# Keys, values and outputs of a delta-rule layer: turned by TensorE, or in 32x32 blocks by VectorE with DMAs through DRAM

## The chip, the cores and the metric

The kernel runs on one core of one Trainium2 chip. The metric is the device time of one execution in microseconds (us). Engines are named as the profile names them: PE (TensorE, matmuls; PEld its weight loads), DVE (VectorE), ACT (ScalarE), POOL (GpSimd) and SP (SyncE, which only issues DMAs here).

## The reference

A decoder trunk of two residual layers on 512 tokens of width 2048, in float32. The first layer is differential attention. The second, which the change touches, is a gated RWKV-7 mixer: 32 heads of 64, each with a 64x64 matrix state that is updated token by token.

```python
p = h @ w_in
p = p + (token_shift(p) - p) * mu
r, k, v, g, dw, da = jnp.split(p, RW_SPLITS, axis=-1)
...
def step(S, inp):
    r_t, w_t, k_t, v_t, a_t, b_t = inp
    sa = jnp.einsum('bhvk,bhk->bhv', S, a_t)
    S = S * w_t[:, :, None, :] + sa[..., None] * b_t[:, :, None, :] + v_t[..., None] * k_t[:, :, None, :]
    y = jnp.einsum('bhvk,bhk->bhv', S, r_t)
    return S, y
...
y = (y - mean) * lax.rsqrt(var + GN_EPS)
y = y * gn_w.astype(F32).reshape(RW_HEADS, RW_HEAD_DIM) + gn_b.astype(F32).reshape(RW_HEADS, RW_HEAD_DIM)
y = y + jnp.sum(rh * kh * r_k.astype(F32), axis=-1, keepdims=True) * vh
y = y.reshape(B, T, RW_WIDTH).astype(h.dtype) * jax.nn.silu(g)
return y @ w_out, v_first
```

## The kernel before

**Precision and projections.** Every large product is three matmuls (`mm3`, line 124) on parts of 32-bit numbers: high x high, high x low, low x high. A weight tile of 512 KB is loaded by SP (`load_w`, line 78) into one of three buffers `wraw`, ScalarE makes the high part `wh` (line 105), VectorE the low part `wl` (line 106), two buffers each, and TensorE runs 24 matmuls with the pair of parts.

**The second layer by pairs.** `layer1` walks over 16 blocks of 128 channels, two heads each, called pairs. In the loop's iteration j four projections run: values of pair j, keys of j + 1, gate of j - 2, receptances of j + 1. Channels lie on the partitions, the 512 tokens along the row. The recurrence is worked in eight chunks of 64 tokens. For a pair, `stage1` and `stage2` make the decays, the queries `AR` and the keys `BK` (its last write is line 1317). `gram` multiplies keys by queries (line 1361) and sends the lower triangles to DRAM (`ltd`, lines 1350 and 1373, on SP). `t_solve` loads them back on the GpSimd queue (`LT`, line 1407) and inverts them by substitution on VectorE (lines 1409 to 1429). The result goes out to `td` (line 1430) and back into `TT` (line 1449), both on SP, is turned in 32x32 blocks by VectorE (`T`, line 1459) and completed by small matmuls (lines 1465 and 1476).

**The chain.** The sequential scan of pair j - 1 (`scan_pair`) runs during iteration j, its matmuls set between those of the projections: each projection matmul counts one `tick`, and after a given number the generator goes one step on. A scan step c, one for each chunk, has three short products (lines 1558, 1569, 1576) with ScalarE copies and a VectorE update between them. At given steps it also calls a function of the dictionary `others`: in the iterations from j = 4 on, at step 0 `turn_keys(p, 0)` and `finish_y` of pair j - 2, at step 1 `turn_keys(p, 4)`, at step 2 `turn_values`; at step 4 and 6 go pieces of pair j's solve, at step 6 also `weigh`, which calls `gated`. After the last step come the outputs (lines 1598, 1602), `centre`, and in the next iteration `group_norm`, which leaves the normed outputs in `yc` and used the buffer `ysq` for squares.

**The three turns.** The scan wants keys, values and outputs with the axes swapped, 128x128 at a time. `turn_keys` makes four TensorE transposes into a PSUM bank (line 1393) and one ScalarE copy into `BKT` (line 1394, two buffers), twice a pair. `turn_values` makes four (line 1502) and four copies into `VS` (line 1506, two buffers). `finish_y` makes four of `yc` (line 1637), and VectorE scales the bank and adds it to `y` (line 1639). `gated` multiplies `y` by the gate (line 1531) and sends it to DRAM.

**What sets the order.** A scheduler puts the instructions of each engine in order, by priority and by when it reckons their inputs to be ready. A priority is the place in the program less an offset: 2000 for weight splits and loads, 3000 for what a chain step calls, 4000 or more for the solve. `issue_after` binds only instructions of the same engine to a place, so chain steps bind their matmuls to the tick, but not their VectorE work or DMAs. Each engine and each DMA queue then works in that fixed order: SP's queue carries the weights, `ltd`, `td` and `TT`, and whatever waits at its head holds up all behind it.

Of the kernel before, what the change touches and what calls it, by code (L numbers as in the profile page):

```python
# [13 lines left out]
F32 = mybir.dt.float32  # L14
# [4 lines left out]
ALU = mybir.AluOpType  # L19
# [4 lines left out]
P = 128  # L24
D = 2048
T = 512
KT = D // P
NT = T // P
# [13 lines left out]
def ahead(offset):  # L42


    def deco(f):
        def g_(g, *a, **k):
            with g.tc.high_priority(offset=offset):
                return f(g, *a, **k)

        return g_  # L50

    return deco
# [1139 lines left out]
C = 64  # L1192
NC_ = T // C
HALF = 32
NG = 4
# [55 lines left out]


class Pair:
    pass


def mus(g, i, j):
# [130 lines left out]
def turn_keys(g, p, c0):  # L1388

    nc = g.nc  # L1390
    ps = g.ps.tile([P, 512], F32, name="pt", tag="pb", bufs=2)
    for i in range(4):
        nc.tensor.transpose(ps[:, i * P : (i + 1) * P], p.BK[:, c0 + i].rearrange("p s t -> p (s t)"), g.ident[:])  # L1393
    nc.scalar.copy(p.BKT[:, c0 : c0 + 4], ps[:].rearrange("p (c k) -> p c k", c=4))


@ahead(SOLVE)
def t_solve(g, j, p, split):


    nc, w = g.nc, g.work
    NQ = HALF // NG
    LT = w.tile([P, HALF + 1, HALF], F32, name="LT", tag="LT", bufs=1)
    Tm = w.tile([P, NQ, HALF], F32, name="Tm", tag="Tm", bufs=1)
    tmp = w.tile([P, NQ * HALF], F32, name="tmpl", tag="tmpl", bufs=1)
    for i in range(NG):
        ld = nc.gpsimd.dma_start(out=LT[i * 32 : i * 32 + 32], in_=g.ltd[j % 2].rearrange("b h c s t -> (b h c) s t"))
    n2 = LT[:, HALF, :]
    nc.vector.tensor_scalar(n2, n2, 1e-24, None, ALU.max)
    nc.vector.reciprocal(n2, n2)  # L1410
    nc.gpsimd.memset(Tm[:], 0.0)
    tf = Tm[:].rearrange("p q t -> p (q t)")
    for i in range(NG):
        nc.gpsimd.memset(tf[i * 32 : i * 32 + 32, i :: HALF + NG], 1.0)

    def steps(a, b):
        for i in range(a, b):
            n, s = HALF - 1 - i, i // NG + 1
            tt = tmp[:, : n * s].rearrange("p (a b) -> p a b", a=s)
            nc.vector.scalar_tensor_tensor(tt, LT[:, i : i + 1, i + 1 :].to_broadcast([P, s, n]), n2[:, i : i + 1],  # L1420
                                           Tm[:, 0:s, i : i + 1].to_broadcast([P, s, n]), ALU.mult, ALU.mult)
            nc.vector.tensor_add(Tm[:, 0:s, i + 1 :], Tm[:, 0:s, i + 1 :], tt)  # L1422

    def parts():
        for a, b in zip(PARTS, PARTS[1:]):
            with g.tc.high_priority(offset=SOLVE), g.tc.issue_after(g.state.ins) if a and split else ExitStack():
                steps(a, b)
                if b == HALF - 1:
                    g.solved = nc.vector.tensor_mul(Tm[:], Tm[:], n2[:, None, :].to_broadcast([P, NQ, HALF])).ins
                    nc.sync.dma_start(out=g.td[j % 2].rearrange("q l t -> l q t"), in_=Tm[:])  # L1430
            if split:
                yield

    p.solve = parts()
    next(p.solve, None)
    return ld.ins
# [91 lines left out]


def gated(g, j, p, gt):  # L1530
    g.nc.vector.tensor_mul(gt[:], gt[:], p.y[:])
    g.nc.gpsimd.dma_start(out=g.yd2[j * P : (j + 1) * P, :], in_=gt[:])

# [85 lines left out]
def group_norm(g, j, p):  # L1619
    p.chain.finish(g)  # L1620
    nc, w, yc = g.nc, g.work, p.yc
    NG = 2 * NT
    sq = w.tile([P, NG, C], F32, name="ysq", tag="ysq", bufs=1)
    nc.scalar.activation(sq[:], yc[:], AF.Square)
    var = g.small.tile([P, NG], F32, name="var", tag="var", bufs=3)
    nc.vector.reduce_sum(var[:], sq[:], AX.X)
    nc.vector.tensor_scalar(var[:], var[:], 1.0 / C, GN_EPS, ALU.mult, ALU.add)
    rs = g.small.tile([P, NG], F32, name="rsg", tag="rsg", bufs=3)
    rsqrt(g, rs[:], var[:], NG, "r8")
    nc.vector.tensor_mul(yc[:], yc[:], rs[:, :, None].to_broadcast([P, NG, C]))  # L1630
# [11 lines left out]
def layer1(g, aps):  # L1642
    nc, tc = g.nc, g.tc
    with ExitStack() as cx:
# [3 lines left out]
        w = g.work  # L1648
        pairs = []
# [26 lines left out]
        r = receptances(0)  # L1676
        for j in range(D // P):
            p = pairs[j]
            if j:
                others = [(0, lambda p=p: turn_keys(g, p, 0)), (1, lambda p=p: turn_keys(g, p, 4)),  # L1680
                          (2, lambda p=p: turn_values(g, p))]
                if j > LAG + 1:
                    others[0] = (0, lambda p=p, i=j - 2: (turn_keys(g, p, 0), finish_y(g, i, pairs[i])))
                elif j > 1:
                    others.append((3, lambda i=j - 2: finish_y(g, i, pairs[i])))
                full = LAG < j < D // P - 1
                if full:
                    others += [(4, lambda p=p: next(p.solve)), (6, lambda p=p: (next(p.solve), weigh()))]
                gaps = ((6, 8) if j > LAG + 1 else (5, 6)) if full else (4, 4) if j > LAG else (4, 5)
                leads = {1: 72, LAG: 18, LAG + 1: 42}  # L1690
                chain(g, j - 1, pairs[j - 1], 5, *gaps, others, leads.get(j, GAP_D - GAP_T)).step(g)
            stage2(g, j, r, p)
            normed = j > LAG + 1 and pairs[j - 2].chain.wait is None
            if normed:
                group_norm(g, j - 2, pairs[j - 2])

            def behind(m, j=j, p=p, normed=normed):
                if j > 1:
                    pairs[j - 2].chain.finish(g)
                with tc.issue_after(m.ins):  # L1700
                    gram(g, j, p, j > LAG + 1 and pairs[j - 1].chain)
                with tc.issue_after(g.lower) if normed else ExitStack():
                    p.rfs = split_act(g, p.rf[:], w, "x")
                mask_gram(g, p, 0)
                loaded = t_solve(g, j, p, LAG < j < D // P - 1)
                with tc.issue_after(loaded):
                    mask_gram(g, p, 1)
                if j > 1 and not normed:
                    group_norm(g, j - 2, pairs[j - 2])

            stage_v(g, j, p, proj(2, j, behind=(24 if j == 1 else 18, behind)))
            if j == 0:
                turn_keys(g, p, 0)
                turn_keys(g, p, 4)
                Chain(g, first_values(g, p), 20)
            if j == 1:
                first = gate_of(0, "g0")
            if j + 1 < D // P:
                begin(j + 1)
            if j > LAG:  # L1720
                weights.append((j - LAG, gate(g, j - LAG, proj(3, j - LAG), later=True)))
            if j + 1 < D // P:
                r = receptances(j + 1)
            weigh()
            if j == LAG:
                gated(g, 0, pairs[0], first)
# [54 lines left out]
        for nm in ("11", "21", "22", "12"):  # L1781
            t, c = PLACES[nm]
# [21 lines left out]
@with_exitstack  # L1804
def body(ctx, tc, nc, aps):
    g = Ctx()
    g.nc, g.tc = nc, tc
    g.last, g.first, g.centred = None, [], None
    g.chains, g.later, g.state, g.copied = [], [], None, None
    g.const = ctx.enter_context(tc.tile_pool(name="const", bufs=1))  # L1810
    g.small = ctx.enter_context(tc.tile_pool(name="small", bufs=2))
    g.hp = ctx.enter_context(tc.tile_pool(name="hp", bufs=16))
    g.wraw = ctx.enter_context(tc.tile_pool(name="wrawp", bufs=3))
    g.wh = ctx.enter_context(tc.tile_pool(name="whp", bufs=2))
    g.wl = ctx.enter_context(tc.tile_pool(name="wlp", bufs=2))
    dr = ctx.enter_context(tc.tile_pool(name="dr", bufs=1, space=DRAM))
    g.ys = [dr.tile([D - 256, T], F32, name=f"ys{i}") for i in range(2)]
    g.yd2 = dr.tile([D, T], F32, name="yd2")
    g.xd = aps["x1"] if "x1" in aps else dr.tile([T, D], F32, name="xd")
    g.ltd = dr.tile([2, 2, 2, NC_, HALF + 1, HALF], F32, name="ltd")  # L1820
    g.td = dr.tile([2, HALF // NG, P, HALF], F32, name="td")
    g.ident = g.const.tile([P, P], F32, name="ident")
    g.fixed = g.const.tile([P, 16], F32, name="fixed")
    g.neglam, g.subw = g.fixed[:, 0:1], g.fixed[:, 1:3]
    make_identity(nc, g.ident)
    for n, layer in ((4, layer0), (2, layer1)):
        with tc.tile_pool(name="pp", bufs=n, space=PSUM) as g.pp, \
                tc.tile_pool(name="ps", bufs=1, space=PSUM) as g.ps:
            layer(g, aps)
# [42 lines left out]
```

## Time and profile before

| | us |
|---|---|
| median of 3 runs | 2054.83 (2054.38 to 2057.75) |
| profiled execution | 2055.6 |
| its span, first to last instruction | 2053.9 |
| PE busy | 2035.2 |
| VectorE busy | 1605.9 |
| ScalarE busy | 1133.6 |
| GpSimd busy | 400.3 |

The second layer's pairs run from about 950 to 1900 us of the span, one pair in some 59 us (line 1393's first transposes of a pair start at 1233.44, 1292.38, 1351.31, ...). How to read the profile: busy time is a sum over instructions of one engine, where overlapping matmuls count once; a row of the groups is "line engine operation out<-in shapes xcount | busy us, mean ns | idle time before them and who ended it"; a row of the timeline is "start us, duration us, engine line operation out<-in xcount [idle before <- releaser]"; a row of the windows has the stretch, its length, each engine's busy time with the number of instructions, the granted clock of TensorE (1.00 is full), the share of the DMA engines' time, and GB/s; a row of one line's instructions has min/median/max in ns, then first and last start. DMA issues by SP have no landing time in this trace; those by GpSimd have one.

### The profile page before, as it was taken

The page shows a single profiled execution, that of the slowest core. Times are in us where ns is not written, and L with a number is a line of the kernel's source. Part 1 is how long each engine was busy: PE and PEld are TensorE (multiplying, and loading weights), DVE is VectorE, ACT ScalarE, POOL GpSimd, SP SyncE. Part 2 cuts the span into 40 slices and gives each one's busy share as a digit, 9 for nine tenths or more (in the row PEclk, how much of TensorE's full clock was granted, in tenths as well). Part 3 has the DMA queues.
Part 4 walks back from the last instruction along what each step waited for, and adds up shares of the span by engine and source line. Part 5 has one row for each costly group of instructions (what it writes and reads, how often), then busy time and mean ns, then how long its engine had stood idle before and what let it go on. Part 6 is the DMA issues. An engine that isn't in the chain of part 4 may idle for free.

```text
span 2053.9 us, 34174 instructions
## 1 busy us (share of the span) xinstructions
PE 2035.2 (99%) x11922; PEld 1673.1 (81%) x11922; DVE 1605.9 (78%) x4100; ACT 1133.6 (55%) x2258; POOL 400.3 (19%) x782
## 2 busy tenths in 40 slices
PE   9999999999999999999999999999999999999999
PEld 7888888888888888888877778888888888877887
DVE  7988988888898977476787888787777888777745
ACT  5765656666666544355565555555555555545423
POOL 1020111102011000121222222322222222231011
PEclk9999999999999999999999999999999999999999
DMA  8487978879787965823333323223333232346676
GB/s 288 156 163 192 182 172 186 164 192 167 190 180 171 274 218 172 175 87 108 103 83 92 94 77 98 92 89 98 98 98 98 87 96 83 111 127 201 212 182 145
DMA packets 159534, 297.76 MB, mean 145 GB/s; under 512 B 64529, under 2 KB 81937, under 8 KB 159361
## 3 DMA queue, kind: packets, MB, share of 16 engines
q1 hardware_dynamic: 110768, 184.39, 28.8%
q0 software_dynamic: 25952, 90.88, 23.2%
q10 hardware_dynamic: 22640, 20.30, 3.1%
q8 instruction: 94, 1.54, 0.3%
q14 instruction: 80, 0.65, 0.1%
HBM read 271.33 MB, written 24.18 MB: 144 GB/s over the span
## 4 chain that ended last, share of the span: by engine, by line
PE 90%; DVE 6%; ACT 2%; issue 1%; DMA 1%; SPq 0%; ACTq 0%; DVEq 0%
PE pp L124 45%; PE pp L574 24%; PE pt L124 5%; PE gp L1361 2%; DVE wl L106 2%; PE sm L1558 1%; PE sc L124 1%; PE o L124 1%; PE sm L1576 1%; PE sm L1569 1%; ACT wh L105 1%; PE Y L1598 1%; PE pt L296 1%; PE z L124 1%; PE pt L1393 1%
## 5 line engine op out<-in xcount | busy, mean ns | idle before, releaser
L106 DVE TENSOR_TENSOR wl<-wraw,wh 128x1024 fp32r<-128x1024 f32 (+1 forms) x286 | 349.7, 1223 | 167.7 <-ACT wh L105 157.0
L105 ACT CAST wh<-wraw 128x1024 fp32r<-128x1024 f32 (+1 forms) x286 | 299.5, 1047 | 237.6 <-PE pp L124 115.8
L124 PE MATMUL pp<-hL,wh 128*128 128x512 f32 x1024 | 413.6, 404 | 0.0
L124 PE MATMUL pp<-hH,wl 128*128 128x512 f32 x1024 | 413.0, 403 | 0.0
L124 PE MATMUL pp<-hH,wh 128*128 128x512 f32 x1024 | 412.3, 403 | 0.2 <-ACT wh L105 0.2
L124 PEld LDWEIGHTS pp<-hH,wh 128*128 128x128 f32 x1024 | 193.1, 189 | 34.5 <-ACT wh L105 0.4
L124 PEld LDWEIGHTS pp<-hL,wh 128*128 128x128 f32 x1024 | 193.1, 189 | 33.5
L124 PEld LDWEIGHTS pp<-hH,wl 128*128 128x128 f32 x1024 | 193.2, 189 | 32.4
L574 PE MATMUL pp<-wh,hH 128*128 128x512 f32 x448 | 176.8, 395 | 0.0
L574 PE MATMUL pp<-wh,hL 128*128 128x512 f32 x448 | 175.8, 392 | 0.0
L124 PE MATMUL pp<-wh,hH 128*128 128x512 f32 x376 | 147.0, 392 | 0.6 <-ACT hH L1147 0.6
L124 PE MATMUL pp<-wl,hH 128*128 128x512 f32 x376 | 147.5, 392 | 0.0
L124 PE MATMUL pp<-wh,hL 128*128 128x512 f32 x376 | 147.3, 392 | 0.1
L1420 DVE SCALAR_TENSOR_TENSOR tmpl<-LT,Tm 128x60 f32<-128x60 f32 (+24 forms) x496 | 134.8, 272 | 13.2
L574 PE MATMUL pp<-wl,hH 128*128 128x512 f32 x448 | 140.3, 392 | 0.0
L1564 POOL COPY SA<-VS 64x64 f32<-64x64 f32 x224 | 55.4, 248 | 397.8 <-DVE VS L1580 375.4
L1422 DVE TENSOR_TENSOR Tm<-Tm,tmpl 128x60 f32<-128x60 f32 (+24 forms) x496 | 103.4, 209 | 11.7
L1561 ACT COPY rhs<-sm 64x64 f32<-64x64 f32 x256 | 53.0, 207 | 84.8 <-PE sm L1558 81.8
L574 PEld LDWEIGHTS pp<-wl,hH 128*128 128x128 f32 x448 | 84.5, 189 | 17.2
L574 PEld LDWEIGHTS pp<-wh,hH 128*128 128x128 f32 x448 | 84.2, 188 | 17.5 <-issue 0.4
L574 PEld LDWEIGHTS pp<-wh,hL 128*128 128x128 f32 x448 | 84.3, 188 | 16.1
L1571 ACT COPY VS<-sm 64x64 f32<-64x64 f32 x256 | 52.9, 207 | 76.2 <-PE sm L1569 70.3
(435 smaller groups left out, 4374.4 us busy)
## 6 DMA issues: line engine op xcount, KB each, us to landing
wraw<-in_rw_w_in_dram SPq DMA_DIRECT2D x128, 512.0 KB
wraw<-in_da_w_in_dram SPq DMA_DIRECT2D x75, 512.0 KB
wraw<-in_da_w_in_dram POOLq DMA_DIRECT2D x28, 512.0 KB, 6.6
wraw<-in_da_w_out_dram SPq DMA_DIRECT2D x26, 512.0 KB
wraw<-in_rw_w_out_dram SPq DMA_DIRECT2D x24, 512.0 KB
Ta<-in_da_w_in_dram POOLq DMA_DIRECT2D x21, 512.0 KB, 5.6
Tb<-in_da_w_in_dram POOLq DMA_DIRECT2D x21, 512.0 KB, 5.7
Tc<-in_da_w_in_dram POOLq DMA_DIRECT2D x21, 512.0 KB, 5.5
```

What stands on the lines that cost most here:

```text
L105: a = nc.scalar.copy(hi[:, ks], raw[:, ks])
L106: d = nc.vector.tensor_sub(lo[:, ks], raw[:, ks], hi[:, ks].bitcast(F32))
L124: m = nc.tensor.matmul(out, a, b, start=s, stop=e, skip_group_check=skip)
L296: nc.tensor.transpose(pt[:, c * P : (c + 1) * P], t1s[t][:, c * P : (c + 1) * P], g.ident[:])
L574: m = nc.tensor.matmul(out[t][:], x, wt[lo][:, k, :], start=first, stop=end and lo == 1 and k == KG - 1, skip_group_check=True)
L1361: m = nc.tensor.matmul(gp[h][:, i * P : (i + 1) * P], BK[r_, c0 + i, :, :], p.AR[r_, c0 + i, :, :], start=True, stop=True)
L1393: nc.tensor.transpose(ps[:, i * P : (i + 1) * P], p.BK[:, c0 + i].rearrange("p s t -> p (s t)"), g.ident[:])
L1420: nc.vector.scalar_tensor_tensor(tt, LT[:, i : i + 1, i + 1 :].to_broadcast([P, s, n]), n2[:, i : i + 1], Tm[:, 0:s, i : i + 1].to_broadca ...
L1422: nc.vector.tensor_add(Tm[:, 0:s, i + 1 :], Tm[:, 0:s, i + 1 :], tt)
L1561: nc.scalar.copy(rhs[r_, :], sm[r_, h * C : h * C + C])
L1564: nc.gpsimd.tensor_copy(p.SA[r_, c - 1, :], VS[r_, c, h, :])
L1571: g.copied = nc.scalar.copy(VS[r_, c, h, :], sm[r_, P : P + C])
```

## The change

In the iterations j = 4 to 15 the three functions are replaced by others that use no TensorE. `send_keys` turns each half of the pair's keys in 32x32 blocks with one VectorE transpose of 128x512, which leaves the blocks themselves at the wrong places. With the second half done, four DMAs on SP write the blocks to their places in a DRAM tile, and a fifth reads the whole back into `BKT`. `send_values` does the same for values (one transpose, four writes, two read-backs into `VS`, with `VS` itself as the buffer of the turned blocks), `send_y` for outputs (one transpose into `ysq`, four writes, one read-back). The writes go in pieces of 32 numbers, 128 bytes. The multiply-add that ended `finish_y` becomes a function `settle`, called at scan step 5, or by `gated` if it was not called until then. Pairs 0 to 3 for keys and values, and 0, 1, 14 and 15 for outputs, stay as before. Step 0 calls the first half of the keys and the outputs, step 1 the second half, step 2 the values.

```diff
+def halves_of(x):
+    return x.rearrange("(b r) t (q k) -> q r t b k", b=4, q=4)
+
+def send_keys(g, j, p, c0):
+    nc = g.nc
+    row = lambda x: x[:, c0 : c0 + 4].rearrange("p c k -> p (c k)")
+    nc.vector.transpose(row(p.BKT), p.BK[:, c0 : c0 + 4].rearrange("p c s t -> p (c s t)"))
+    if c0:
+        for q in range(4):
+            nc.sync.dma_start(out=halves_of(g.bkd[j % 2])[q],
+                              in_=p.BKT[q * 32 : q * 32 + 32].rearrange("r c (b k) -> r c b k", b=4))
+        nc.sync.dma_start(out=p.BKT[:], in_=g.bkd[j % 2])
+
+def send_values(g, j, p):
+    nc = g.nc
+    p.VS = g.work.tile([P, NC_, 2, C], F32, name="VS", tag="VS", bufs=2)
+    turned = p.VS[:].rearrange("p c h n -> p (c h n)")[:, 0:T]
+    nc.vector.transpose(turned, p.v[:])
+    for q in range(4):
+        nc.sync.dma_start(out=g.vd[j % 2, q // 2].rearrange("(b r) c (n k) -> n r c b k", b=2, n=2)[q % 2],
+                          in_=turned[q * 32 : q * 32 + 32].rearrange("r (c b k) -> r c b k", c=NC_, b=2))
+    for h in range(2):
+        nc.sync.dma_start(out=p.VS[(1 - h) * C : (2 - h) * C, :, h, :], in_=g.vd[j % 2, h])
+
+def send_y(g, j, p):
+    nc = g.nc
+    flat_ = lambda x: x[:].rearrange("p g n -> p (g n)")
+    nc.vector.transpose(flat_(p.sq), flat_(p.yc))
+    for q in range(4):
+        nc.sync.dma_start(out=halves_of(g.ytd[j % 2])[q],
+                          in_=flat_(p.sq)[q * 32 : q * 32 + 32].rearrange("r (t b k) -> r t b k", t=NT, b=4))
+    nc.sync.dma_start(out=flat_(p.sq), in_=g.ytd[j % 2].rearrange("p t k -> p (t k)"))
+
+    def settle():
+        p.settle = None
+        nc.vector.scalar_tensor_tensor(p.y[:], flat_(p.sq), g.prm["hgw"][:, j : j + 1], p.y[:], ALU.mult, ALU.add)
+
+    p.settle = settle
...
 def gated(g, j, p, gt):
+    if p.settle:
+        p.settle()
     g.nc.vector.tensor_mul(gt[:], gt[:], p.y[:])
...
                 if j > LAG + 1:
-                    others[0] = (0, lambda p=p, i=j - 2: (turn_keys(g, p, 0), finish_y(g, i, pairs[i])))
+                    others = [(0, lambda p=p, i=j - 2: (send_keys(g, i + 2, p, 0), send_y(g, i, pairs[i]))),
+                              (1, lambda p=p, j=j: send_keys(g, j, p, 4)), (2, lambda p=p, j=j: send_values(g, j, p)),
+                              (5, lambda i=j - 2: pairs[i].settle and pairs[i].settle())]
...
+    g.bkd = dr.tile([2, P, NC_, P], F32, name="bkd")
+    g.vd = dr.tile([2, 2, C, NC_, C], F32, name="vd")
+    g.ytd = dr.tile([2, P, NT, P], F32, name="ytd")
```

More of the change, by code (lines that the diff above doesn't have):

```diff
@@ L1253 @@
 class Pair:
-    pass
+    settle = None
 def mus(g, i, j):
@@ L1622, in group_norm @@
     NG = 2 * NT
-    sq = w.tile([P, NG, C], F32, name="ysq", tag="ysq", bufs=1)
+    sq = p.sq = w.tile([P, NG, C], F32, name="ysq", tag="ysq", bufs=1)
     nc.scalar.activation(sq[:], yc[:], AF.Square)
```

## The prediction

> **What bounds the kernel now.** I read the page first: busy time by engine and the chain that ended last.
>
> ```profile
> span 2053.9 us, 34174 instructions
> PE 2035.2 (99%) x11922; PEld 1673.1 (81%) x11922; DVE 1605.9 (78%) x4100; ACT 1133.6 (55%) x2258; POOL 400.3 (19%) x782
> ...
> PE 90%; DVE 6%; ACT 2%; issue 1%; DMA 1%; SPq 0%; ACTq 0%; DVEq 0%
> ```
>
> TensorE works in 99% of the span and carries 90% of the chain. A page's average may hide stages, so next come the windows, cut at one pair's period inside the changed stretch (1174 to 1822 us, where pairs 4 to 15 are prepared).
>
> ```profile
> 1292.00:1351.00 59.00, 59.00 (x428) 48.90 (x427) 46.51 (x129) 32.75 (x75) 15.00 (x37) 1.00 0.32 95
> ```
>
> In this 59 us the columns are PE 59.00, weight loads 48.90, VectorE 46.51, ScalarE 32.75, GpSimd 15.00, granted clock 1.00, DMA share 0.32. TensorE never rests; every other engine has room. Time taken off TensorE here should come off the kernel, as long as nothing new stops it.
>
> How much is that time? The busy time of overlapping matmuls is modelled, so I go by starts in TensorE's timeline. First a scan step without transposes, then three steps of one pair with them: step 0 (keys' first half and outputs), step 1 (keys' second half), step 2 (values).
>
> ```profile
> 1204.38 0.38 PE L1576 MATMUL sm<-VS,BKT 128*128 128x128 f32 x2
> 1204.52 0.48 PE L124 MATMUL pp<-hL,wh 128*128 128x512 f32 x1
> ...
> 1233.22 0.38 PE L1576 MATMUL sm<-VS,BKT 128*128 128x128 f32 x2
> 1233.44 0.60 PE L1393 MATMUL pt<-ident,BK 128*128 128x128 f32 x4
> 1233.88 0.60 PE L1637 MATMUL pt<-ident,yc 128*128 128x128 f32 x4
> 1234.23 0.48 PE L124 MATMUL pp<-hH,wl 128*128 128x512 f32 x1
> ...
> 1239.85 0.49 PE L1393 MATMUL pt<-ident,BK 128*128 128x128 f32 x3
> 1240.18 0.39 PE L1576 MATMUL sm<-VS,BKT 128*128 128x128 f32 x2
> ...
> 1240.43 0.47 PE L124 MATMUL pp<-hL,wh 128*128 128x512 f32 x1
> ...
> 1245.57 0.41 PE L1576 MATMUL sm<-VS,BKT 128*128 128x128 f32 x2
> 1245.82 0.60 PE L1502 MATMUL pt<-ident,mixv 128*128 128x128 f32 x4
> 1246.17 0.48 PE L124 MATMUL pp<-hH,wh 128*128 128x512 f32 x1
> ```
>
> Without transposes the projection follows the state product by 0.14 us (1204.38 to 1204.52). With eight it follows by 1.01 (1233.22 to 1234.23), which is 0.87 more. In step 1 the sequence takes 0.58 from the first transpose (1239.85 to 1240.43) where 0.14 would do: 0.44. In step 2 it takes 0.60: 0.46.
>
> **The change part by part.**
>
> *TensorE loses the transposes.* In the iterations j = 4 to 15 all sixteen of a pair go: eight of keys and four of values of pair j, four of outputs of pair j - 2. By the starts that is 0.87 + 0.44 + 0.46 = 1.77 us a pair, and 12 x 1.77 = 21.2 us. The other end is the busy sum:
>
> ```profile
> L1393 PE MATMUL pt<-ident,BK 128*128 128x128 f32 x128 | 20.7, 273 | 0.0
> L1637 PE MATMUL pt<-ident,yc 128*128 128x128 f32 x64 | 9.7, 274 | 1.0 <-DVE yc L1630 1.0
> L1502 PE MATMUL pt<-ident,mixv 128*128 128x128 f32 x64 | 9.6, 272 | 0.0
> ```
>
> 96 of 128, 48 of 64 and 48 of 64 go, three quarters of 40.0 us: 30.0. I take 21.2, because a start-to-start difference is what the next matmul really waited, while the busy sum counts overlap with it. 30.0 stays as the far end of the gain.
>
> *VectorE gains four transposes of 128x512 a pair,* two for keys, one each for values and outputs. The trace has one of 64x256, and a cheap small operation:
>
> ```profile
> L1459 DVE STREAM_TRANSPOSE T<-TT x32: 425/440/443, 1003.3 to 1868.1; 64x256 f32<-64x256 f32 x32
> ...
> L1409 DVE TENSOR_SCALAR LT<-LT x16: 172/181/183, 963.4 to 1831.2; 128x32 f32<-128x32 f32 x16
> ...
> L1639 DVE SCALAR_TENSOR_TENSOR y<-pt,prm_hgw,y x16: 742/751/752, 1079.7 to 1916.7; 128x512 f32<-128x512 f32 x16
> ```
>
> From 32 to 256 elements a row the time grows by 440 - 181 = 259 ns, 1.16 ns an element; 256 more give 440 + 296 = 736 ns (estimate). Bounds: 440 (if the row's length cost nothing) and 880 (if all of it did). So 4 x 0.74 = 2.9 us a pair, between 1.8 and 3.5. The multiply-add of the outputs (L1639, 0.75 us) stays on VectorE, reads SBUF for PSUM and moves to step 5. VectorE goes from 46.5 to 49.4 us busy in a period that shrinks from about 59 to 57.2: 86%. Cost on the path: none as long as splits and solve (below) stay ahead; at worst all of it, 12 x 2.9 = 35 us.
>
> ```profile
> L1394 ACT COPY BKT<-pt x32: 576/588/597, 961.0 to 1826.8; 128x512 f32<-128x512 f32 x32
> ...
> L1506 ACT COPY VS<-pt x64: 364/367/370, 966.0 to 1831.8; 64x256 f32<-64x256 f32 x64
> ```
>
> *ScalarE loses these PSUM copies* of keys (2 of 588 ns) and values (4 of 367), 2.6 us a pair. It is not the bound: worth 0, and no loss, since nothing is added there.
>
> *SP gains 16 DMAs a pair:* five for keys, six for values, five for outputs, each group four writes in 128-byte pieces and read-backs that must wait for all four. They stand in one queue with the projection weights, with the solve's `ltd`, `td` and `TT`. Its issues take about 0.45 us each (TT below, 1.95 for four), 7 us of a 57 us period. Bounds: 0.35 each, or, if a three-dimensional pattern were cut up fourfold, some 29 us, which still fits. This is one turn of the solve's way through SP:
>
> ```profile
> 1271.12 0.43 DVE L1429 TENSOR_TENSOR Tm<-Tm,LT 128x256 f32<-128x256 f32 x1
> ...
> 1271.61 0.39 SPq L1430 DMA_DIRECT2D td<-Tm  x1
> 1272.50 0.35 SPq L78 DMA_DIRECT2D wraw<-in_rw_w_in_dram  x1
> 1275.20 1.95 SPq L1449 DMA_DIRECT2D TT<-td  x4
> ...
> 1276.16 0.76 DVE L1613 TENSOR_REDUCE s<-Y 128x4 f32<-128x256 f32 x2 [1.95 <-PE Y L1602]
> ...
> 1278.04 0.91 DVE L1459 STREAM_TRANSPOSE T<-TT 64x256 f32<-64x256 f32 x2 [0.25 <-DMA TT<-td]
> ...
> 1283.38 0.69 PE L1465 MATMUL px<-T,G 32*32 32x32 f32 x32
> ...
> 1288.49 1.05 ACT L105 CAST wh<-wraw 128x1024 fp32r<-128x1024 f32 x1 [0.26 <-ACT TT L1479]
> ```
>
> A write in 128-byte pieces with its read-back behind it is already there: td, 128 KB, issued at 1271.61, lets TT go at 1275.20, after 3.6 us. The rate of such writes, from windows of half a microsecond (last column GB/s):
>
> ```profile
> 1272.50:1273.00 0.50, 0.50 (x5) 0.46 (x4) 0.50 (x2) 0.41 (x2) 0.00 (x0) 1.00 1.21 207
> ...
> 1288.00:1288.50 0.50, 0.50 (x4) 0.40 (x3) 0.00 (x0) 0.24 (x2) 0.50 (x2) 1.00 0.40 66
> ...
> 1289.50:1290.00 0.50, 0.50 (x4) 0.41 (x3) 0.43 (x1) 0.45 (x3) 0.00 (x0) 1.00 0.40 65
> ```
>
> td runs at 207 GB/s, the four small `ltd` writes at 66. So the keys' 512 KB take 2.5 to 7.9 us, values and outputs (256 KB) 1.3 to 4.0 each. I take the middle, 5 and 2.6: td's form is nearest (one big write), but here come four smaller ones. A round trip is then some 10 us for keys and 8 for the others, with td's 3.6 us as pattern, waiting included.
>
> Who waits behind that on SP? The weights. The load issued at 1272.50 fills the buffer that is split at 1288.49, after those of two other buffers: 16.0 us later. A 512 KB load lands in 6.6 us on the queue for which the page has it:
>
> ```profile
> wraw<-in_da_w_in_dram POOLq DMA_DIRECT2D x28, 512.0 KB, 6.6
> ```
>
> So SP can stand still for 9.4 us before a split is late. One blocked read-back (up to 8 us if the order puts it directly behind its writes) is covered. If that cover were gone, the price would be the rest of it, 0 to 2 us a blocked read-back. I count 0.
>
> *The consumers.* Keys and values are wanted one period after they are sent: covered. The outputs are wanted at step 5. Steps come every (1245.57 - 1233.22) / 2 = 6.2 us, so step 5 is 31 us behind step 0, against some 8 for the round trip. VectorE waits there only if its queue has the multiply-add much earlier.
>
> *The solve* is the tight place. Its result T ends at 1278.95 and TensorE wants it at 1283.38: 4.4 us of slack. Removing 1.8 us of TensorE's work ahead of that leaves 2.7. VectorE's work inside the solve grows by the values' transpose and the multiply-add of outputs, 0.74 + 0.75 = 1.5, which leaves 1.2. The start of the solve has slack too:
>
> ```profile
> LT<-ltd POOLq DMA_DIRECT2D x64, 132.0 KB, 4.5
> ...
> 1291.00 2.09 POOL L1407 DMA_DIRECT2D LT<-ltd  x4 [1.50 <-DMA ltd<-G]
> ...
> 1300.29 0.18 DVE L1409 TENSOR_SCALAR LT<-LT 128x32 f32<-128x32 f32 x1
> ```
>
> LT's issue ends at 1293.1; a load of LT lands in 4.5 us, so they are there near 1297, 3 us ahead of use. One period already shows T late:
>
> ```profile
> 1224.48 0.69 PE L1465 MATMUL px<-T,G 32*32 32x32 f32 x30 [2.00 <-DVE T L1459]
> ```
>
> That stall of 2.0 us once in twelve is what I price for the tight place: one more like it, +2.0, between -2.0 (the old one goes) and the whole gain.
>
> *Sum,* against the profiled execution, 2055.6 us (span 2053.9 and 1.7 around it): 2055.6 - 21.2 + 2.0 = 2036.4. The median of the runs is 0.8 below that execution: 2035.6. I forecast 2036.
>
> **The Trainium skill** on this: "DMA: Bandwidth & Descriptors", Specifications, asks for 512 bytes or more a transfer; smaller ones are read, modified and written. If each 128-byte piece cost as much as 512 at the 207 GB/s seen, the keys would take 10 us for my 5. The `ltd` rows (66 GB/s) go some way to that, td's row does not.
>
> **The rivals.**
>
> *A. The key writes get ahead of TT (slower).* Both keys' transposes can run once the pair's keys are made, before the gram products, and a chain step's priority lets them go early. VectorE idles for 1.95 us up to 1276.16, just there. If the four key writes stand in SP's queue ahead of TT at 1275.2, T comes later by 1.6 (issue) + 2.5 to 7.9, say 6.5, with 1.5 from the solve: 8.0 against 4.4 - 1.8 = 2.7. TensorE then stands 5.3 us a pair: 12 x 5.3 = 64, less 21: 2099. It decides from 4.4 us of delay on (stall equal to the gain). For it: the place and the shared queue. Against: TT comes from an earlier step with the same priority, and is ready about when the key transposes are.
>
> *B. The gain is eaten, no change.* The solve is 3 to 4.5 us later through VectorE alone (all added transposes inside it, or a wait for outputs), TensorE stands 1.8 us a pair: 2055. For it: VectorE would be 86% busy. Against: two of the four transposes fit into gaps like the 1.95 us one.
>
> *C. Strided DMA as such is too slow.* If the pieces went 19 times slower than 207 GB/s, a pair's 1 MB written would take 96 us against a period of 57, and the kernel would be near 2055 + 12 x 37 = 2500. The td and `ltd` rows speak against it. The factor is from "VectorE: DVE Perf Modes", The three transpose paths, a rule for copies whose inner stride is large, which also advises TensorE for 128x128; here the inner run is 32 elements in a row, and the trace does not agree.
>
> *D. The transposes cost TensorE nothing,* as they lie under weight loads. Then 2055. The starts above exclude nearly all of it.
>
> **How the numbers follow.** Forecast with its smaller losses 0.73; A 0.15; B 0.07; C 0.02; D 0.01; some other loss of the size of A 0.02. The forecast's own range is 2029 (a gain 7 us above 21.2, most of the way to 30.0) to 2048 (a stall of 1 us in every pair). Range for 8 in 10: 2029 to 2056, which takes in B and D and leaves out A and C. A measurement of this kernel tells 0.2%, 4 us, from no change. Faster 0.73, same 0.08, slower 0.19.
>
> **What would show it.** Right: TensorE stays at 99% in the windows of pairs 4 to 15 with a period near 57.2; the groups L1393, L1502, L1637 shrink to a quarter; stream transposes of 128x512 near 0.74 us; TensorE's wait for T (L1465) below 3 us in total. Wrong: a wait at L1465 or at the first product of a scan step in every pair (A or B), VectorE waiting for the read-back of outputs, splits waiting for weights, or a period that stays at 59 with TensorE busy (D).

## The result, and the profile after

The change makes the kernel slower: median 2218.82 us (2217.20 to 2222.07, 4 runs) against 2054.61 of before on the same chip (2053.91 to 2057.75, 4 runs), ratio 1.0798, 95% interval 1.0779 to 1.0817. The forecast was 2036.

The page of the kernel after: span, TensorE's busy time, the chain that ended last.

```profile
span 2215.5 us, 34114 instructions
PE 2118.0 (96%) x11730; PEld 1679.3 (76%) x11730; DVE 1638.1 (74%) x4148; ACT 1104.3 (50%) x2186; POOL 434.7 (20%) x782
...
PE 19%; DVE 8%; DMA 2%; ACT 2%; issue 1%; POOL 0%; SPq 0%; ACTq 0%; POOLq 0%; DVEq 0%
```

TensorE went from 99% to 96% of a longer span: it waits now. The chain's 19% cannot be set against the 90% of before: this chain goes back only to 1480.7 us, and its shares, which are of the whole span, add up to about a third. TensorE's modelled busy time even grew (2035.2 to 2118.0) with 192 matmuls fewer, so busy time alone says little here. The view of waits, cut to the changed pairs of the kernel after (columns: engine, line, what ended the wait; us in total, times, longest), shows where:

```profile
PE pp L124 <- DVE mixk L1188: 19.1, 7, 3.9
PE px L1511 <- DVE T L1505: 11.7, 6, 2.8
PE pp L124 <- ACT wh L105: 7.7, 7, 3.6
PE pp L124 <- DVE mixv L1188: 7.6, 1, 7.6
PE pp L124 <- DVE wl L106: 6.8, 4, 2.9
```

No line stands out, and the sum is far below the 164 us lost. When a long ring of engines is late all round, TensorE's own waits can each be small and name none of them. One period of the kernel after shows the ring. The rows are SP's, with those of the other engines that bear on it, in order of time (L1455 is the solve's first operation, L1476 sends its result, L1187 is ScalarE's first step on the next pair's values, L1373 the solve's four tiles on SP, L1453 their load on GpSimd's queue):

```profile
1586.95 0.14 DVE L1455 TENSOR_SCALAR LT<-LT 128x32 f32<-128x32 f32 x1
...
1614.04 0.38 SPq L1476 DMA_DIRECT2D td<-Tm  x1
...
1616.14 0.62 POOL L1580 DMA_DIRECT2D yd<-mixv  x1 [18.76 <-DVE mixv L1579]
1616.26 1.87 SPq L1495 DMA_DIRECT2D TT<-td  x4
...
1621.05 0.69 ACT L1187 ACTIVATE mixv<-pp,omu 128x512 f32<-128x512 f32 x1 [7.96 <-DMA yd<-mixv]
...
1623.29 2.59 SPq L1420 DMA_DIRECT2D vd<-VS  x4
...
1629.17 1.23 SPq L1423 DMA_DIRECT2D VS<-vd  x2
...
1631.11 2.19 SPq L1373 DMA_DIRECT2D ltd<-G  x4
...
1647.94 2.00 POOL L1453 DMA_DIRECT2D LT<-ltd  x4
...
1657.53 0.14 DVE L1455 TENSOR_SCALAR LT<-LT 128x32 f32<-128x32 f32 x1
```

From one solve's start to the next it is 70.6 us (1586.95 to 1657.53). The solve itself is not slower: it ends when td leaves, 27.1 us after its start. But the next pair's tiles leave only 17.1 us behind td, after the values' read-back, and their load comes 16.8 us later still, behind scan copies on GpSimd. Each solve hangs on the one before. The link that closes the ring is ScalarE's largest wait (view of waits of ScalarE, 1174 to 1960 us):

```profile
ACT mixv L1187 <- DMA yd<-mixv: 79.2, 10, 9.9
```

The gate of one pair and the values of the next use one buffer, `mixv`. The gate's last steps are bound behind the solve's end, `settle` comes between them, and only when their store `yd` has landed can ScalarE write the next values. These have to be turned, sent and read back before the next tiles leave. In the pairs of before (1174 to 1822 us) this wait does not occur. In the timeline of before the same tiles go out as soon as their small rows (L1350) are gone:

```profile
1285.20 1.08 SPq L1350 DMA_DIRECT2D ltd<-ssl  x2
1287.18 1.81 SPq L1373 DMA_DIRECT2D ltd<-G  x4
...
1291.00 2.09 POOL L1407 DMA_DIRECT2D LT<-ltd  x4 [1.50 <-DMA ltd<-G]
```

### The profile page after: what moved, and what is told of

Read it like the earlier page. It is cut to its first block, busy times and chain, and to the rows that moved or that the text cites. A ratio compares the mean times of both kernels' runs of the same rounds, so it can differ in the third digit from the quotient of the medians.

```text
span 2215.5 us, 34114 instructions
## 1 busy us (share of the span) xinstructions
PE 2118.0 (96%) x11730; PEld 1679.3 (76%) x11730; DVE 1638.1 (74%) x4148; ACT 1104.3 (50%) x2186; POOL 434.7 (20%) x782
## 5 line engine op out<-in xcount | busy, mean ns | idle before, releaser
L124 PE MATMUL pp<-hH,wh 128*128 128x512 f32 x1024 | 422.3, 412 | 34.7 <-DVE mixk L1188 19.1
L124 PE MATMUL pp<-hH,wl 128*128 128x512 f32 x1024 | 423.8, 414 | 7.1 <-DVE wl L106 6.8
L124 PE MATMUL pp<-hL,wh 128*128 128x512 f32 x1024 | 420.3, 410 | 0.0
L124 PEld LDWEIGHTS pp<-hH,wh 128*128 128x128 f32 x1024 | 198.2, 194 | 75.1 <-DVE mixk L1188 22.1
L124 PEld LDWEIGHTS pp<-hH,wl 128*128 128x128 f32 x1024 | 197.9, 193 | 44.0 <-DVE wl L106 10.0
L1466 DVE SCALAR_TENSOR_TENSOR tmpl<-LT,Tm 128x60 f32<-128x60 f32 (+24 forms) x496 | 140.2, 283 | 10.9
L1612 POOL COPY SA<-VS 64x64 f32<-64x64 f32 x224 | 86.0, 384 | 304.9 <-DVE VS L1628 220.7
L1628 DVE SCALAR_TENSOR_TENSOR VS<-sm,gam,Sg 64x64 f32<-64x64 f32 x192 | 54.3, 283 | 100.1 <-PE sm L1624 93.0
```

What stands on the lines that cost most here:

```text
L124: m = nc.tensor.matmul(out, a, b, start=s, stop=e, skip_group_check=skip)
L1612: nc.gpsimd.tensor_copy(p.SA[r_, c - 1, :], VS[r_, c, h, :])
L1628: g.state = nc.vector.scalar_tensor_tensor(VS[r_, c + 1, h, :], s_, p.gam[r_, c : c + 1], Sg[r_, :], ALU.mult, ALU.add)
```

## The experiments

Two causes are to be told apart, and each has a rival. **Theory 1:** VectorE's added work costs time, in one stretch of the pair. **Theory 2:** the new DMAs cost time by their places in SP's one fixed queue. Rival to 1: TensorE alone sets the pace. Rival to 2: the transfers, in 128-byte pieces, crowd out others.

**e1: the solve's tiles early on SP.** In `gram`, for all pairs:

```diff
-    with g.tc.high_priority(offset=SOLVE if j == D // P - 1 else 0):
+    with g.tc.high_priority(offset=SOLVE):
```

> One edit to the changed kernel: the four writes ltd<-G of each pair get the solve's priority (4000) where they had none, so on SP they no longer stand behind the new DMAs. Theory (order on SP): in the changed kernel ltd<-G leaves 47 us after the gram products (1584.0 to 1631.1), so each solve starts late and hangs on the one before it; here it leaves within 10 us of them, the period falls from 70 us to 57 to 60, and the time to 2030 to 2065 us. Rival 1 (contention: the 128-byte pieces slow all transfers): the pieces are all still there, so 2150 us or more. Rival 2 (VectorE: four transposes and the later multiply-add lengthen the solve): the solve starts early but ends late, 2120 us or more.

Measured: 2227.45 us, ratio 1.0836 (1.0818 to 1.0854). A miss. The tiles did go out early, yet TensorE now waits for the splits of weights (view of waits of TensorE, then one row of each of SP's and ScalarE's timelines, e1):

```profile
PE pp L124 <- ACT wh L105: 96.6, 11, 9.8
PE pp L124 <- DVE wl L106: 41.4, 11, 5.5
...
1625.02 1.11 SPq L78 DMA_DIRECT2D wraw<-in_rw_w_in_dram  x2
...
1629.57 1.04 ACT L105 CAST wh<-wraw 128x1024 fp32r<-128x1024 f32 x1 [6.29 <-DMA wraw<-in_rw_w_in_dram]
```

Here the loads are late: none leaves SP between 1586.6 and 1625.0 us, while the new DMAs do, and ScalarE waits for the one of 1625.02. One wait of 8.8 us a pair (96.6 / 11) took the place of the ring. To mend one victim of the queue is not enough.

**e2, e3: values alone, outputs alone.** The rest keeps TensorE's transposes:

```diff
 e2
+    others = [(0, lambda p=p, i=j - 2: (turn_keys(g, p, 0), finish_y(g, i, pairs[i]))),
+              (1, lambda p=p, j=j: turn_keys(g, p, 4)), (2, lambda p=p, j=j: send_values(g, j, p))]
 e3
+    others = [(0, lambda p=p, i=j - 2: (turn_keys(g, p, 0), send_y(g, i, pairs[i]))),
+              (1, lambda p=p, j=j: turn_keys(g, p, 4)), (2, lambda p=p, j=j: turn_values(g, p)),
...
```

> Only values go the new way; keys and outputs are turned by TensorE as before. In this program ltd<-G stands on SP right behind the writes of ssl, ahead of the new DMAs. Theory (order on SP): nothing is late, and four transposes are gone from 12 pairs: 2054.6 - 12 x 0.46 = 2049 us (2043 to 2054). Rivals 1 and 2 (contention, VectorE): a quarter of the pieces and of the transposes should cost about a quarter of the loss of 164 + 21 us: 2090 to 2100 us.

> Only outputs go the new way. On SP ltd<-G now stands behind TT, the four writes of the outputs, two weight loads and the read-back of the outputs. Theory (order on SP): ltd<-G leaves 10 to 20 us later than before, more than the 3 us that LT is ahead of its use: slower, 2070 to 2150 us. Rivals 1 and 2: a quarter of the loss, 2090 to 2100 us, with ltd<-G at its old distance from the gram products.

Measured: e2 2062.19 us, ratio 1.0033 (1.0020 to 1.0046), between its two expectations. The view of waits of e2 has TensorE a little late behind VectorE's scan updates, 20 times:

```profile
PE sm L1606 <- DVE VS L1628: 4.0, 20, 0.2
```

e3 measured 2104.45 us, ratio 1.0237 (1.0221 to 1.0252), in the range of theory 2, but close to the rivals' 2090 to 2100 too. What decides is the place of the tiles for the solve: they stand on SP right behind the outputs' read-back and leave 16.4 us after the start of the gram products (1415.73 to 1432.12), where before has 2.8 (1284.36 to 1287.18).

**e4: everything by VectorE, no DMA.** The 12 writes and four read-backs of a pair go; keys become zeros, and the values are turned by two transposes where the change has one.

```diff
-        for q in range(4):
-            nc.sync.dma_start(out=halves_of(g.bkd[j % 2])[q], ...
-        nc.sync.dma_start(out=p.BKT[:], in_=g.bkd[j % 2])
+        nc.gpsimd.memset(p.BKT[:], 0.0)
...
```

> The changed kernel without its DMAs: the four transposes on VectorE and the multiply-add at step 5 stay. Left out is the placing of the blocks, so the output is not the reference's; BKT is set to zero by GpSimd after the two transposes of keys (which keeps the numbers finite), and the values are turned by two transposes of 64x512 where the change has one of 128x512. Theory (order on SP) and rival 1 (contention) both expect the whole of TensorE's gain here: 2054.6 - 21 = 2034 us (2026 to 2045). Rival 2 (VectorE) expects most of the loss to stay: 2120 us or more.

Measured: 2063.81 us, ratio 1.0040 (1.0026 to 1.0053). Neither theory alone gave that. Of the 164 us some 155 hang on the DMAs; but without any of them TensorE's saving does not show either. So there is a second loss at least as large as the saving; whether it is VectorE's is asked next.

**e5, e6: four extra VectorE transposes, in two places.** Before, plus four unread 128x512 transposes a pair. In e5 they stand among the solve's steps, in e6 right behind the normed outputs:

```diff
+def turn_again(g, p):
+    with g.tc.high_priority(offset=SOLVE), g.tc.issue_after(g.state.ins):   # e5 only
+        g.nc.vector.transpose(flat_(p.sq), flat_(p.yc))
...
+    others += [(3, again), (4, lambda ...: (next(p.solve), again())), (5, again), (6, ...)]   # e5
+    others: two at step 0, one at step 1, one at step 2                                       # e6
```

> The kernel before with TensorE's transposes and ScalarE's copies kept, and in each of the 12 pairs four more 128x512 transposes by VectorE whose result nobody reads (the normed output into the tile of its squares), one behind each of four scan updates that stand among the steps of the solve. Nothing else is added and the output stays the reference's. Theory 1, VectorE sets the pace in the solve: each costs its own 0.72 us, 4 x 0.72 x 12 = 35 us, so 2080 to 2100. Rival, TensorE alone sets the pace, as the prediction had it: 2050 to 2062.

> The same four unread transposes a pair as in the run before it, but all four right behind the normed output, between the end of one solve and the first step of the next, where VectorE's row of the kernel before has some 5 us idle. Theory 1, VectorE sets the pace in the solve alone: 2053 to 2065. Rival, VectorE's time counts wherever it is spent, or its transposes slow another engine: 2080 to 2100.

Measured: e5 2083.25 us, ratio 1.0133 (1.0118 to 1.0148), 28 us more than before; e6 2056.05, ratio 1.0005 (0.9995 to 1.0014). The same work costs 28 us in one place and nothing in the other. 28 / 48 = 0.58 us each, 83% of the 0.70 that the change's transposes take. The windows of before, cut at the solve instead of at the whole pair, had it all along (fifth column VectorE):

```profile
1284.40:1300.30 15.90, 15.90 (x138) 13.71 (x135) 7.93 (x15) 9.34 (x24) 7.70 (x14) 1.00 0.35 98
1300.30:1330.50 30.20, 30.20 (x151) 24.90 (x150) 28.25 (x90) 19.16 (x46) 6.22 (x16) 1.00 0.20 67
```

VectorE is busy 28.25 of 30.20 us in the solve, 94%, and 7.93 of 15.90, 50%, in the stretch before it. Its mean of 78% describes neither.

**e7, e8: the same transfers in two orders.** e7 is e4 with the 16 DMAs back as traffic that waits for nothing (the expectation's 18 is a slip), behind the solve's tiles. e8 is the complete change in another order on VectorE and SP.

```diff
 e7 and e8, and for the writes and read-backs of keys, values (e7) and outputs
+        with g.tc.issue_after(g.kept):            # the last of the solve's four tiles
...
 e8
+    with g.tc.issue_after(g.solved):              # keys' transposes, settle
+        nc.vector.transpose(row(p.BKT), ...)
...
+    send_keys(g, j, p, 0); send_keys(g, j, p, 4); send_y(g, j - 2, pairs[j - 2])   # behind t_solve
+    send_values(g, j, p)                                                           # behind stage_v
+    others = [(3, lambda p=p, j=j: (take_keys(g, j, p), pairs[j - 2].take()))]     # read-backs
```

> The kernel of e4 (all transposes by VectorE, keys replaced by zeros, values turned by two 64x512 transposes, normed outputs left in 32x32 blocks: not the reference's output), and the change's 18 DMAs a pair put back as traffic alone: the 12 scattered writes of the same shapes read tiles that are long there, and the four read-backs are copies of the same sizes from a weight block into DRAM, so that none waits for anything and nobody waits for it; on SP they stand right behind the solve's four tiles, which go out as soon as they are made. Theory 2, the loss comes of what SP's one queue holds up (waiting read-backs, tiles of the solve and weights issued late): 2055 to 2085, near e4's 2064. Rival, the transfers themselves crowd out weights and solve tiles in the DMA engines: 2120 or more, up to the change's 2219.

> The change itself, keys, values and outputs, output the reference's, in another order: key and output transposes on VectorE behind the end of the solve before, the value's right when the values are made, on SP the tiles for the solve first and every new write behind them, read-backs one scan step or more behind their writes, the multiply-add that settles the output behind the solve's end. If theories 1 and 2 hold, both losses go and TensorE's saving of up to 21 us shows: 2030 to 2060. If the transfers themselves cost (rival to 2) it stays at 2120 or more; if VectorE's added work counts anywhere (rival to 1) 2065 to 2090.

Measured: e7 2176.89 us, ratio 1.0595 (1.0580 to 1.0611), as the rival to 2 had it; but e8 2070.08, ratio 1.0071 (1.0054 to 1.0088), which excludes that rival as the price of the transfers as such. The writes are the same in number, size and pieces. Their places on SP differ. The timeline of SP in e7:

```profile
1369.02 1.79 SPq L1373 DMA_DIRECT2D ltd<-G  x4
1370.85 2.63 SPq L1438 DMA_DIRECT2D ytd<-hH  x4
...
1374.26 4.45 SPq L1410 DMA_DIRECT2D bkd<-AR  x4
...
1384.13 23.92 SPq L78 DMA_DIRECT2D wraw<-in_rw_w_in_dram  x5
```

and in e8, one period:

```profile
1347.83 1.81 SPq L1373 DMA_DIRECT2D ltd<-G  x4
1349.69 0.64 SPq L1410 DMA_DIRECT2D bkd<-BKT  x1
1351.48 0.35 SPq L78 DMA_DIRECT2D wraw<-in_rw_w_in_dram  x1
1351.87 0.62 SPq L1410 DMA_DIRECT2D bkd<-BKT  x1
```

In e7 sixteen issues in a row keep SP for 13 us (1370.85 to 1384.1), 0.8 us each, and the first weight load comes 15.1 us behind the tiles; in e8 weights and writes alternate and it comes 3.7 us behind them. TensorE in e7 then stands for a split (rows of ScalarE, VectorE and TensorE, then two windows, e7):

```profile
1398.15 1.98 ACT L105 CAST wh<-wraw 128x1024 fp32r<-128x1024 f32 x2
...
1405.35 2.35 DVE L106 TENSOR_TENSOR wl<-wraw,wh 128x1024 fp32r<-128x1024 f32 x2
...
1406.62 0.79 PE L124 MATMUL pp<-hH,wl 128*128 128x512 f32 x1 [6.65 <-DVE wl L106]
...
1394.00:1398.00 4.00, 3.88 (x20) 2.93 (x19) 3.79 (x14) 2.54 (x8) 1.03 (x1) 1.00 0.00 0
1398.00:1402.00 4.00, 0.73 (x2) 0.30 (x2) 3.80 (x12) 2.13 (x3) 1.32 (x3) 0.80 0.01 2
```

But this stall is not one for a load that is still under way. The DMA engines are idle from 1394 on (shares 0.00 and 0.01), ScalarE makes the high part without a wait, and the low part, on VectorE, starts 6 us after the first high part is done: it stands there behind steps of the solve. All ten long stalls of TensorE in e7 (6.6 to 6.7 us each, with the DMA engines idle throughout) are of this kind. So in e7 the lost time shows in the order on VectorE, which the scheduler laid out with SP's order, and no row shows the transfers or a late load holding TensorE there. That no read-back needs to wait for such a loss, e7 does show; why the scheduler put the splits so late is open.

**e9, e10: the better order with its last losses out.** e9 is e8 with TensorE's transposes kept for values and in the last pair; e10 turns the values on VectorE behind their own solve.

```diff
-                if j > LAG + 1:
+                if LAG + 1 < j < D // P - 1:                       # e9, e10
...
+    if LAG + 1 < j < D // P - 1:
+        send_values(g, j, p)                                       # e10, in t_combine behind TT's DMAs
```

> The order of the run e8 with two edits: values stay with TensorE's transposes, and the last pair keeps the form of before (so 11 pairs for keys and outputs). Both theories of e5 to e8 (VectorE's idle place is free; a read-back or write on SP costs only where solve tiles or weights stand behind it) give 11 x (0.87 + 0.44) = 14 us less than before: 2036 to 2048. If e8's extra 15 us come of the DMAs and not of the value's transpose and the last pair, it stays at 2055 to 2072.

> As the run before it, and the values too are turned by VectorE, but behind the end of their own pair's solve instead of right after they are made, with their six DMAs behind the solve's last blocks on SP. If they come back in time for the scan, 11 x 1.77 = 19 us less than before: 2032 to 2045. If not, the scan's first product waits for the values, some 2 to 5 us a pair: 2060 to 2100.

Measured: e9 2065.71 us, ratio 1.0051 (1.0037 to 1.0065), in the range that was given for a loss by the DMAs; e10 2070.69, ratio 1.0077 (1.0065 to 1.0090), in the range for values that come back late. Both miss the gain, and neither cause is shown: in e10 TensorE waits for no read-back (its largest wait is 4.8 us in 14 times, for VectorE's scan updates). The timeline of ScalarE in e9 shows another reason:

```profile
1361.65 0.72 ACT L1552 ACTIVATE y<-y,prm_hgb 128x512 f32<-128x512 f32 x1 [2.16 <-DVE y L1551]
1362.28 0.42 ACT L1633 COPY VS<-sm 64x64 f32<-64x64 f32 x2
```

The scan's copies stand behind an activation nobody needs yet, and that waits for VectorE.

**e11: the change with its DMAs on GpSimd's queue.** Nothing else is edited (`nc.sync` becomes `nc.gpsimd` in the three functions).

> The change itself with one edit: its 18 DMAs a pair are issued by GpSimd's queue instead of SP's; what VectorE does stays in the change's places. SP's order is then that of before. Theory 2 (SP's one queue is the place): the loss of some 155 us between e4 and the change goes and about VectorE's 10 to 30 us stay, 2060 to 2095, unless GpSimd's own waiting read-backs now hold the scan's copies and the loads of the solve, which would show as waits at those lines: up to 2150. Rival (the transfers themselves): 2180 to 2220.

Measured: 2090.04 us, ratio 1.0169 (1.0155 to 1.0183), inside theory 2's range. The same 16 DMAs (not 18), read-backs with their waits and all, cost 129 us less than on SP. This is the plainest run for theory 2: most of the loss comes of their place in SP's queue, and of the order on the other engines that follows from it. What is left shows as waits for VectorE (view of waits, e11):

```profile
PE sm L1606 <- DVE VS L1628: 18.6, 17, 2.3
PE px L1511 <- DVE T L1505: 9.0, 15, 1.1
```

**e12: e9 with the activation behind the copies.**

```diff
-    nc.scalar.activation(p.y[:], p.y[:], AF.Identity, bias=col("hgb"))
+    g.later.append((1, lambda: nc.scalar.activation(p.y[:], p.y[:], AF.Identity, bias=col("hgb"))))
```

> The run e9 with one edit: ScalarE's activation that adds the bias to the product y comes behind the copies of the next scan step instead of ahead of them. In e9 these copies came 2.7 us after the product they read (1362.3 against 1358.9 and its own 0.3), behind that activation, which waited for VectorE, and the first step of the solve stood 17.0 us behind the Gram matrices where before had 15.9. Theory: e9's missing 2 us a pair are this place, half or all of it: 2040 to 2058. Rival: they are VectorE's lateness in the solve whatever ScalarE does: 2060 to 2068.

Measured: 2056.72 us, ratio 1.0006 (0.9997 to 1.0015): 9 us better than e9, in the theory's range, and no different from before. No version here beats before.

## Why the prediction was wrong, point by point

*TensorE's saving, 1.77 us a pair.* The transposes are gone as counted, but the saving never came out as time, not even in e12, where the 14 us of keys and outputs should show. The step assumed that what TensorE sheds comes off the period. In e12 TensorE still waits for scan updates in the solve, once in each of eight pairs (view of waits, 1280 to 1760 us), and by starts it loses more than that view counts as idle. These are the projection and the scan's first product behind it, in before and then in e12:

```profile
PE sm L1624 <- DVE VS L1646: 4.0, 8, 0.5
...
1318.80 0.40 PE L124 MATMUL pp<-hH,wl 128*128 128x512 f32 x1
1319.03 0.39 PE L1558 MATMUL sm<-VS,G 128*128 128x128 f32 x2
...
1319.63 0.39 PE L124 MATMUL pp<-hH,wl 128*128 128x512 f32 x1
1320.52 0.46 PE L1624 MATMUL sm<-VS,G 128*128 128x128 f32 x2 [0.50 <-DVE VS L1646]
```

Before has 0.23 us from start to start, e12 0.89. Over one pair of e12 (1290.8 to 1349.6 us) the scan's first products come 0.11, 0.08, 0.66 and 0.24 us later than 0.23 behind the projection, 1.1 us in all; in one pair of before it is 0.1. That difference, 1.0 us, is most of the 1.3 us a pair that are missing: VectorE's solve takes back most of what TensorE sheds. It also answers rival D: the transposes did cost TensorE time, which now goes into waiting. Whether another order would let the gain out stays open; no run here tried it.

*VectorE's transposes, 0.74 us each, "none on the path as long as splits and solve stay ahead".* The size was right, as the rows of one of the three lines after show:

```profile
L1430 DVE STREAM_TRANSPOSE ysq<-yc x12: 698/703/711, 1168.4 to 1957.8; 128x512 f32<-128x512 f32 x12
```

The place failed. The window of 59 us gave VectorE 79%; the solve's 30 us would have given 94%, and e5 and e6 show that this is what decides. Its bound (35 us at worst) was good: e5 measured 28. Rival B named this loss, and its 2055 is within 0.5% of e2 and e4, but it had a chance of only 0.07, and the change itself lost far more.

*SP's 16 DMAs, "I count 0".* This is the step that turned the sign. The text listed `ltd`, `td` and `TT` as neighbours in the queue and then checked the cover of the weights alone, for a single blocked read-back, against 9.4 us of slack. Whether the solve's tiles would still leave on time was never asked: before, they leave 2 us behind their rows, with no priority to keep them there, and LT was ready 3 us ahead of use. After, they leave behind td, TT and the values' read-back. Against the 0 that was counted, e11 beside the change puts 129 us on this queue. e1 shows that the weights are the next victim (a wait of up to 9.8 us in each pair). The issue time was sized at 0.45 us where these writes take 0.65 (2.59 for four above) and up to 1.1 (4.45 for four in e7).

*The solve, +2.0.* Wrong in place too. The prediction watched T against TensorE (4.4 us of slack); that wait is 11.7 us in all of the changed pairs. The time went at the solve's start, which it had checked only for a load that leaves on time. Nor did it ask what hangs on the solve's end: the gate's store, whose buffer the next values need. ScalarE's wait for it is 79.2 us in the change and 4.1 in e11, where SP's queue is free of the new DMAs.

*ScalarE's copies, the outputs' 31 us.* Right: VectorE waits for the outputs' read-back once, 0.2 us. No run sets the copies apart.

*Rival A* had the right kind (a new DMA ahead of a DMA of the solve on SP) and the wrong neighbour: TT goes out 2.2 us behind td (1614.04 to 1616.26), no later than before. *Rival C* is refuted by e8, which moves all the pieces within 1% of before. The Trainium skill's rule in "DMA: Bandwidth & Descriptors", Specifications (512 bytes or more a transfer for the full rate) did not decide here for the same reason: the change's 128-byte pieces are in e8 (2070 us) and in e11 (2090 us).

## What to carry to other kernels

Before a step moves from the bounding engine to one with a mean of 78%, cut the windows at that engine's own stages: the price of the added work is that of the stage where it lands, here 0.58 us or 0 for the same instruction. Before DMAs are added to a queue with a fixed order, list every DMA that can come to stand behind them, with its slack, the ones without priority first. A ring of small waits shows in the period between two equal instructions, and in the waits of all engines, not in those of the bounding engine alone. And an order is part of the kernel: with the same 16 transfers a pair it took 2219 us (the change), 2090 (e11) or 2070 (e8).

## What the runs showed of the hardware

The granted clock fell after long stalls. Windows of the kernel after (third column from the end is the clock):

```profile
1392.00:1396.00 4.00, 2.07 (x10) 1.35 (x8) 3.23 (x5) 0.00 (x0) 1.35 (x6) 1.00 0.71 124
1396.00:1400.00 4.00, 0.00 (x0) 0.00 (x0) 0.00 (x0) 0.00 (x0) 0.00 (x0) 0.66 0.89 266
1400.00:1404.00 4.00, 2.34 (x6) 1.86 (x7) 3.14 (x5) 3.86 (x6) 0.00 (x0) 0.50 0.02 3
1404.00:1408.00 4.00, 4.00 (x12) 2.70 (x11) 0.78 (x2) 0.11 (x1) 0.00 (x0) 0.56 0.65 136
1408.00:1412.00 4.00, 4.00 (x75) 2.92 (x73) 0.69 (x1) 2.02 (x5) 1.37 (x3) 1.00 0.91 257
```

TensorE stands from 1394.07 to 1401.66 us. The clock goes to 0.66, then 0.50, and is back at 1.00 only in the window from 1408. In e7 it went to 0.50 in the same way, from 1402 to 1410 us. The second window also shows the ring at its worst: every engine idle, the DMA engines 89% busy. Behind this stall the projections start 0.43 us apart (1402.68 to 1403.11), where 0.23 is usual in this run (1618.14 to 1618.37). Such a stall is thus paid a second time, in slow matmuls behind it; a busy time of TensorE that grows while its work shrinks fits that. A shorter stall, 1621.47 to 1623.64, left the clock at 1.00.
